# Full-block transposes, stacked low-rank products and bound chunk products in a flow-matching step

## The chip, the cores and the metric

The kernel runs on one core of one Trainium2 chip. A core has five engines that work side by side, each with its own queue in fixed order: TensorE (PE; its weight loads are listed as PEld), VectorE (DVE), ScalarE (ACT), GpSimd (POOL) and SyncE (SP, which here only issues DMAs). Products are written to PSUM, in banks; in this kernel VectorE or ScalarE copies them from there. The metric is the device time of one execution in microseconds, the median of three runs.

## The reference

One layer of a hybrid backbone on 640 tokens (512 latent ones around 128 context ones, d = 2048), all in fp32:

```
h = rmsnorm(x) * (1 + sc1) + sh1
p = h @ w_in                      # 2048 x 5408
r, k, v, wd, ad, gd = split(shift(p[..., :3360]))     # wd, ad: 64 wide, gd: 160 wide
gate  = sigmoid(gd) @ g2                              # 160 x 1024
for d in (forward, backward):
    decay = exp(-exp(-softplus(-(w0[d] + tanh(wd) @ w2[d])) - 0.5))   # 64 x 1024
    a     = sigmoid(a0[d] + ad @ a2[d])                               # 64 x 1024
    S     = S * decay + (S @ a_t) b_t + v_t k_t       # 16 heads, state 64 x 64
    out  += group_norm(S @ r_t) + (r . kd) v
o_a = out * gate
o_b = chunk_gmlp(gelu(p[..., 3360:]))
x = x + g1 * (concat(o_a, o_b) @ w_out)
x = x + g2 * (silu(h2 @ w_ffn_gate) * (h2 @ w_ffn_up)) @ w_ffn_down
```

The two outputs are the normalised streams, a third the final states of the context scan. The recurrence over time is done in chunks of 64 tokens.

## The kernel before

Activations lie with features on the 128 partitions and the 640 tokens along the row; halves of 320 tokens go to one PSUM bank. The wide products are taken as fp32r in three passes: each operand is split into a rounded part (hi, a cast on ScalarE, line 164) and the rest (lo, a subtraction on VectorE, line 165), and hi.hi, hi.lo and lo.hi are added up in PSUM (`win`, lines 186 to 188). Small products stay fp32, and each of those is two MATMUL instructions.

The input projection goes over 42 blocks of 128 output columns. First come the three low-rank blocks (wd and ad, then the two gate blocks), then for each pair of heads p (8 pairs) the blocks r, v and k, with gMLP blocks between some pairs. After each block, `take` copies it out and gives its follow-up work to a Mixer, a list of generators that `between` advances in small steps while the next block's products are written. The yields carry estimated costs; solve and merge (inversion of the small triangular matrices inside the chunks) have Mixers of their own. The framework then puts all instructions of an engine in order at build time: an instruction earlier in the program goes first if its operands are ready by the framework's own timing estimate, and otherwise a later one does. On the chip, each queue runs in that order and waits where the estimate was wrong. DMAs for weights, scratch and results are issued by SP, those of solve and merge by POOL.

`low_rank` (line 467) leaves tanh(wd) in rows 0 to 63 and ad in rows 64 to 127 of `wa`, and the sigmoid of the gate blocks in `gs1` (128 rows) and `gs2` (32 rows). `take_k` (line 514) does, for a pair and for each direction d: the low-rank products of `wl` with `wa` (line 551; h = 0 is w2 with tanh(wd) on rows 0 to 63, h = 1 is a2 with ad on rows 64 to 127), the decays, and the operands R and X of the ten chunks, 64 rows for each of the two heads. Then the products inside the chunks, X by R for each chunk and head (line 613, groups of 4, 4 and 2 chunks, one PSUM tile for each head), which are copied out as GB (ScalarE), GR and GA (VectorE, masked). GR goes to the scratch `d_S`. Then X is transposed for each head (line 630, 64 rows to 128 by 64) and stored to `d_S`, and GA by Z is formed (line 641). All PSUM tiles of this work come from the pool `pk`, tag `g`, two buffers.

The recurrence (`recur`) then walks over the chunks of all pairs in an order written out by hand in hops, the second half of the output projection (`wout_b`) filling in. `finish` normalises a pair's output, forms the gate product (`pmm` with g2, line 1196, its matmul at line 485) and stores the result to `d_o`. The first half of the output projection and the FFN follow, which the change does not touch.

## Time and profile before

| | us |
|---|---|
| median of 3 runs | 3431.64 (3423.08 to 3435.26) |
| profiled execution, span from the first to the last instruction | 3424.7 |
| TensorE busy | 3259.0 (95%) |
| VectorE busy | 2478.4 (72%) |
| ScalarE busy | 1443.5 (42%) |
| GpSimd busy | 1260.5 (37%) |
| mean granted TensorE clock | 0.975 |

The page tells the time between the first and the last instruction of one execution; what lies around it is not in the page, and the runs' times hold both. A matmul's listed length holds its way through the array, so that consecutive ones overlap: what one costs is the distance to the start of the next. "xcount" behind a group is the number of instructions, "64*128" the rows and columns of the array that are used, and "<-" names what ended the wait before it.

### The profile page before, as it was taken

How to read it: one execution, taken by the hardware profiler on the slowest of the kernel's cores; microseconds unless marked ns; L12 is line 12 of the kernel's file. 1: busy time of each engine (PE TensorE's matmuls, PEld its weight loads, DVE VectorE, ACT ScalarE, POOL GpSimd, SP SyncE). 2: the span in 40 equal slices, each digit the busy share in tenths (PEclk: the TensorE clock that was granted, in tenths of full speed). 3: DMA queues.
4: the chain of work that ended last, by engine and by line, in shares of the span. 5: the costliest groups of instructions: out<-in, count | busy, mean ns of one | idle time of the engine just before them, and what ended most of it. 6: DMA issues, size and time to landing. Idle time of an engine off the chain costs nothing.

```text
span 3424.7 us, 72654 instructions
## 1 busy us (share of the span) xinstructions
PE 3259.0 (95%) x28260; PEld 2930.6 (86%) x28260; DVE 2478.4 (72%) x4320; ACT 1443.5 (42%) x3161; POOL 1260.5 (37%) x1090
## 2 busy tenths in 40 slices
PE   6899999999999999989999999999999999999996
PEld 3687778777877887768999999999999999999986
DVE  4547677766866666655788788887888877877787
ACT  3334344444444433324644444444444445443365
POOL 0001112122213112231045656666565554555543
PEclk8899999999999999989999999999999999999998
DMA  8666676677667577635634343434434355543453
GB/s 320 232 189 184 178 194 170 186 189 190 192 179 195 147 236 225 208 111 150 182 109 123 107 127 111 120 115 120 122 105 127 116 166 155 154 145 116 144 169 114
DMA packets 736177, 550.12 MB, mean 161 GB/s; under 512 B 140328, under 2 KB 670008, under 8 KB 727000
## 3 DMA queue, kind: packets, MB, share of 16 engines
q1 hardware_dynamic: 723512, 531.78, 52.2%
q0 software_dynamic: 9984, 13.13, 1.9%
q8 instruction: 222, 3.64, 0.4%
q14 instruction: 123, 1.01, 0.1%
q10 hardware_dynamic: 2336, 0.57, 0.1%
HBM read 436.68 MB, written 111.28 MB: 160 GB/s over the span
## 4 chain that ended last, share of the span: by engine, by line
PE 43%; DVE 5%; issue 4%; DMA 2%; ACT 1%; POOL 0%; DVEq 0%; ACTq 0%; POOLq 0%; SPq 0%
PE P L1502 14%; PE P L1500 13%; PE P L1501 13%; DVE lo L1319 2%; DMA d_os<-act 1%; DVE act L1621 1%; DMA opd<-d_op 1%; PE big L1355 0%; DVE xd L1553 0%; PE big L1353 0%; PE big L1354 0%; DVE out L1856 0%; PE C L1434 0%; PE C L1432 0%; PE C L1433 0%
## 5 line engine op out<-in xcount | busy, mean ns | idle before, releaser
L1502 PE MATMUL P<-xo,lo 128*128 128x320 f32 x2352 | 731.4, 311 | 10.2 <-DVE lo L1319 10.2
L1500 PE MATMUL P<-xo,hi 128*128 128x320 f32 x2352 | 728.3, 310 | 2.1 <-ACT hi L1318 2.1
L1501 PE MATMUL P<-xo,hi 128*128 128x320 f32 x2352 | 727.6, 309 | 0.0
L1319 DVE TENSOR_TENSOR lo<-raw,hi 128x512 fp32r<-128x512 f32 x532 | 567.7, 1083 | 82.8 <-ACT hi L1318 78.0
L1318 ACT CAST hi<-raw 128x512 fp32r<-128x512 f32 x532 | 326.7, 621 | 416.0 <-PE P L1501 322.6
L186 PE MATMUL big<-h_hi,hi 128*128 128x320 f32 x1376 | 452.0, 329 | 8.4 <-ACT hi L164 4.3
L1502 PEld LDWEIGHTS P<-xo,lo 128*128 128x128 f32 x2352 | 442.4, 188 | 17.7 <-DVE lo L1319 17.5
L188 PE MATMUL big<-h_hi,lo 128*128 128x320 f32 x1376 | 441.2, 321 | 4.4 <-DVE lo L165 4.4
L1500 PEld LDWEIGHTS P<-xo,hi 128*128 128x128 f32 x2352 | 442.7, 188 | 3.0 <-ACT hi L1318 2.7
L1501 PEld LDWEIGHTS P<-xo,hi 128*128 128x128 f32 x2352 | 442.4, 188 | 0.0
L187 PE MATMUL big<-h_lo,hi 128*128 128x320 f32 x1376 | 438.9, 319 | 0.5 <-DVE h_lo L343 0.5
L1413 POOL TENSOR_TENSOR raw<-raw 128x512 f32<-128x512 f32 x252 | 409.2, 1633 | 10.9 <-DVE lo L1319 0.9
L1502 PE MATMUL P<-xd,lo 128*128 128x320 f32 x1232 | 384.7, 312 | 17.4 <-DVE lo L1319 17.2
L1500 PE MATMUL P<-xd,hi 128*128 128x320 f32 x1232 | 383.0, 311 | 6.0 <-ACT hi L1318 4.2
L1501 PE MATMUL P<-xd,hi 128*128 128x320 f32 x1232 | 381.6, 310 | 0.0
L165 DVE TENSOR_TENSOR lo<-raw,hi 128x512 fp32r<-128x512 f32 x268 | 184.7, 692 | 235.2 <-ACT hi L164 218.8
L186 PEld LDWEIGHTS big<-h_hi,hi 128*128 128x128 f32 x1376 | 265.0, 193 | 83.2 <-issue 54.1
L164 ACT CAST hi<-raw 128x512 fp32r<-128x512 f32 x268 | 164.9, 618 | 311.2 <-PE big L187 129.5
L188 PEld LDWEIGHTS big<-h_hi,lo 128*128 128x128 f32 x1376 | 265.0, 193 | 20.9 <-issue 8.3
L187 PEld LDWEIGHTS big<-h_lo,hi 128*128 128x128 f32 x1376 | 265.1, 193 | 12.9 <-issue 8.3
L1318 ACT CAST hi<-rawd 128x512 fp32r<-128x512 f32 (+1 forms) x288 | 168.9, 588 | 242.1 <-PE P L1501 206.8
L1413 POOL TENSOR_TENSOR t<-raw 128x512 f32<-128x512 f32 x84 | 135.3, 1611 | 344.8 <-DMA raw<-in_w_ffn_up_dram 334.7
(358 smaller groups left out, 6430.1 us busy)
## 6 DMA issues: line engine op xcount, KB each, us to landing
wt<-in_w_mod_dram SPq DMA_DIRECT2D x96, 1024.0 KB
raw<-in_w_ffn_gate_dram SPq DMA_DIRECT2D x182, 256.0 KB
raw<-in_w_ffn_up_dram SPq DMA_DIRECT2D x182, 256.0 KB
rec<-d_S SPq DMA_DIRECT2D x80, 576.0 KB
raw<-in_w_in_dram SPq DMA_DIRECT2D x172, 256.0 KB
rawd<-in_w_ffn_down_dram SPq DMA_DIRECT2D x128, 256.0 KB
raw<-in_w_out_dram SPq DMA_DIRECT2D x96, 256.0 KB
xd<-d_os SPq DMA_DIRECT2D x66, 320.0 KB
```

Of the source, the lines that this page charges most:

```text
L164: S.copy(hi, raw)
L165: V.tensor_sub(lo, raw, hi.bitcast(F32))
L186: TE.matmul(halves[hf], hi[:, k, :], h_hi[:, kb, s], start=(kb == 0), stop=False)
L187: TE.matmul(halves[hf], hi[:, k, :], h_lo[:, kb, s], start=False, stop=False)
L188: TE.matmul(halves[hf], lo[:, k, :], h_hi[:, kb, s], start=False, stop=(kb == KB - 1))
L1318: S.copy(hi[:, 0:nk], raw[:, 0:nk])
L1319: V.tensor_sub(lo[:, 0:nk], raw[:, 0:nk], hi[:, 0:nk].bitcast(F32))
L1413: G.tensor_tensor(out=o[:, 0:nk], in0=p[:, 0:nk], in1=q[:, 0:nk], op=ALU.subtract)
L1500: TE.matmul(ps, hi[:, k, :], xk[:, 0, :], start=f, stop=False)
L1501: TE.matmul(ps, hi[:, k, :], xk[:, 1, :], start=False, stop=False)
L1502: TE.matmul(ps, lo[:, k, :], xk[:, 0, :], start=False, stop=l)
L1621: V.tensor_sub(lo, src, hi.bitcast(F32))
```

## The change

Four places are changed, all around the head-pair work.

1. The products inside the chunks are issued with the heads alternating (second head first), and each group's instructions are tied to one another in that order (`chain`, an ordering without a semaphore). The PSUM pool gets two tags `g0` and `g1` with one buffer each, in place of one tag with two buffers, so that a head always has the same bank.
2. X is transposed for both heads at once, a full 128 by 128 block per chunk, in groups of 4, 4 and 2 chunks, and stored with one DMA per group.
3. The low-rank products become fp32r products over 128 rows: `waM[:, h]` holds the rounded rows of h in one half and the rest of them in the other half, the weight is loaded twice, once for each half, and is split into `wh` and `wl`; two products then give hi and lo parts of both. The weights are loaded and split for each direction.
4. The gate rows go to the scratch `d_gs`, and come back at the start of the recurrence, split into `gh`, `gl` and `gq` (four copies of the last 32 rows, in two of which the rest stands in place of the rounded value). The gate product is four fp32r products for each half. `J2` (the flipped identity) is made there too, and the solve's input `gi` gets a tile of its own.

```diff
+    d_gs = dp.tile([160, T], F32, name="d_gs")
...
+    def chain(made):
+        for a, b in zip(made, made[1:]):
+            tc.add_manual_dep(b.ins, a.ins.name, mybir.DependencyInfo(
+                mybir.DependencyClass.NoSync, mybir.DependencyReason.DATA), reason="chain")
...
-    wa = bk.tile([P, T], F32, name="wa", bufs=1)
+    waM = bk.tile([P, 2, T], F32R, name="waM", bufs=1)
...
         if b == 24:
-            S.activation(wa[0:64, :], z[0:64, :], AF.Tanh)
-            S.copy(wa[64:128, :], z[64:128, :])
+            S.activation(z[0:64, :], z[0:64, :], AF.Tanh)
+            zl = z.bitcast(F32R)
+            for h in range(2):
+                S.copy(waM[hsl(h), h, :], z[hsl(h), :])
+                V.tensor_sub(zl[hsl(h), :], z[hsl(h), :], waM[hsl(h), h, :].bitcast(F32))
+                nc.sync.dma_start(waM[osl(h), h, :].bitcast(F32), z[hsl(h), :])
         else:
-            dst = gs1 if b == 25 else gs2
-            S.activation(dst, z, AF.Tanh, scale=0.5)
-            V.tensor_scalar(dst, dst, 0.5, 0.5, op0=ALU.mult, op1=ALU.add)
+            S.activation(z, z, AF.Tanh, scale=0.5)
+            V.tensor_scalar(z, z, 0.5, 0.5, op0=ALU.mult, op1=ALU.add)
+            nc.sync.dma_start(d_gs[0:P] if b == 25 else d_gs[P:160], z)
...
-        wl = bk.tile([P, 2, P], F32, tag="wl", name="wl", bufs=1)
-        nc.sync.dma_start(wl[0:64, :, :], w2[0, :, :, p * P:(p + 1) * P].rearrange("d k n -> k d n"))
-        nc.sync.dma_start(wl[64:128, :, :], a2[0, :, :, p * P:(p + 1) * P].rearrange("d k n -> k d n"))
+        def load_wl(d):
+            raw = bk.tile([P, 2, P], F32, tag="GR", name="wlr", bufs=2)
+            for h, w in enumerate((w2, a2)):
+                nc.sync.dma_start(raw[:, h, :], w[0, d, :, p * P:(p + 1) * P].unsqueeze(0).to_broadcast([2, 64, P]))
+            yield 0.5
+            wh, wl = (bk.tile([P, 2, P], F32R, tag=n, name=n, bufs=1) for n in ("wh", "wl"))
+            S.copy(wh, raw)
+            V.tensor_sub(wl, raw, wh.bitcast(F32))
+            o.wl = wh, wl
+            yield 0.5
+        yield from load_wl(0)
...
-                two = [pk.tile([P, HALF], F32, tag="g", name="pwa") for _ in range(2)]
+                two = [pk.tile([P, HALF], F32, tag=f"g{h}", name="pwa") for h in range(2)]
                 for h in range(2):
-                    TE.matmul(two[h], wl[hsl(h), d, :], wa[hsl(h), s], start=True, stop=True)
+                    for i, w in enumerate(o.wl):
+                        TE.matmul(two[h], w[:, h, :], waM[:, h, s], start=i == 0, stop=i == 1)
...
+            if d == 0:
+                yield from load_wl(1)
...
-                two = [pk.tile([P, 4, P], F32, tag="g", name="pG") for _ in range(2)]
-                for cc in range(c0, c1):
-                    for h in range(2):
-                        s = hsl(h)
-                        TE.matmul(two[h][:, cc - c0, :], X[s, cc, :, :].rearrange("p s t -> p (s t)"),
-                                  R[s, cc, :, :].rearrange("p s t -> p (s t)"), start=True, stop=True)
+                two = [pk.tile([P, 4, P], F32, tag=f"g{h}", name="pG") for h in range(2)]
+                chain([TE.matmul(two[h][:, cc - c0, :], X[hsl(h), cc, :, :].rearrange("p s t -> p (s t)"),
+                                 R[hsl(h), cc, :, :].rearrange("p s t -> p (s t)"), start=True, stop=True)
+                       for cc in range(c0, c1) for h in (1, 0)])
...
-            for (c0, c1) in ((0, 8), (8, NCH)):
-                two = [pk.tile([P, 8, CH], F32, tag="g", name="pXT") for _ in range(2)]
+            for (c0, c1) in ((0, 4), (4, 8), (8, NCH)):
+                ps = pk.tile([P, 4, P], F32, tag=f"g{c0 // 4 % 2}", name="pXT")
                 for cc in range(c0, c1):
...
+                    TE.transpose(ps[:, cc - c0, :], X[:, cc, :, :].rearrange("p s t -> p (s t)"), ident)
+                XT = bz.tile([P, 4, P], F32, tag="XT", name="XT", bufs=2)
+                S.copy(XT[:, 0:c1 - c0, :], ps[:, 0:c1 - c0, :])
+                yield 0.2 * (c1 - c0)
+                nc.sync.dma_start(d_S[p, :, d, c0:c1, F_X:F_X + P], XT[:, 0:c1 - c0, :])
...
-    pk = pbx.enter_context(tc.tile_pool(name="pk", bufs=2, space=PSUM))
+    pk = pbx.enter_context(tc.tile_pool(name="pk", bufs=1, space=PSUM))
...
+        gh, gl, gq = (rw.tile([P, T], F32R, name=n) for n in ("gh", "gl", "gq"))
+        nc.sync.dma_start(gl.bitcast(F32), d_gs[0:P])
+        S.copy(gh, gl.bitcast(F32))
+        V.tensor_sub(gl, gl.bitcast(F32), gh.bitcast(F32))
+        gr = rw.tile([P, T], F32, tag="sq", name="gr")
+        for k in range(4):
+            nc.sync.dma_start(gr[32 * k:32 * k + 32, :], d_gs[P:160])
...
-            nc.sync.dma_start(g2a, g2[0, 0:P, p * P:(p + 1) * P])
-            nc.sync.dma_start(g2b, g2[0, P:160, p * P:(p + 1) * P])
+            nc.sync.dma_start(g2r[:, 0, :], g2[0, 0:P, p * P:(p + 1) * P])
+            for k in range(4):
+                nc.sync.dma_start(g2r[32 * k:32 * k + 32, 1, :], g2[0, P:160, p * P:(p + 1) * P])
...
-            pmm([(g2a, gs1), (g2b, gs2)],
...
+            S.copy(g2h, g2r)
+            V.tensor_sub(g2l, g2r[:, 0, :], g2h[:, 0, :].bitcast(F32))
+            V.tensor_sub(g2h[64:128, 1, :], g2r[64:128, 1, :], g2h[64:128, 1, :].bitcast(F32))
...
+                four = ((g2h[:, 0, :], gh), (g2h[:, 0, :], gl), (g2l, gh), (g2h[:, 1, :], gq))
+                for i, (l, r) in enumerate(four):
+                    TE.matmul(ps, l, r[:, s], start=i == 0, stop=i == 3)
```

More of the change, by code (lines that the diff above doesn't have):

```diff
@@ L623, in take_k @@
                     nc.sync.dma_start(d_S[p, :, d, c0:c1, F_G + CH * h:F_G + CH * h + CH], GR[:, 0:c1 - c0, :])
[L625 to L626 removed]
+            for (c0, c1) in ((0, 4), (4, 8), (8, NCH)):
+                ps = pk.tile([P, 4, P], F32, tag=f"g{c0 // 4 % 2}", name="pXT")
                 for cc in range(c0, c1):
[L628 to L636 removed]
+                    TE.transpose(ps[:, cc - c0, :], X[:, cc, :, :].rearrange("p s t -> p (s t)"), ident)
[3 more added lines that the diff above has]
+                nc.sync.dma_start(d_S[p, :, d, c0:c1, F_X:F_X + P], XT[:, 0:c1 - c0, :])
             for c0 in (0, 5):
[L638 removed]
+                ps = pk.tile([P, 5, CH], F32, tag=f"g{1 - c0 // 5}", name="pW0")
                 for cc in range(c0, c0 + 5):
@@ L746, in solve @@
         o = pairs[p]
-        gi = mix[0:80, 0:512].rearrange("p (d a b) -> p d a b", d=2, b=16)
+        gi = gi_
         for d in range(2):
```

39 lines of the change are left out of this document (18 added, 21 removed).

## The prediction

> **What bounds the kernel now.** I read the page first, then busy time by stretch, then TensorE's groups, and last the spacing of single instructions.
>
> ```profile
> span 3424.7 us, 72654 instructions
> PE 3259.0 (95%) x28260; PEld 2930.6 (86%) x28260; DVE 2478.4 (72%) x4320; ACT 1443.5 (42%) x3161; POOL 1260.5 (37%) x1090
> PE 43%; DVE 5%; issue 4%; DMA 2%; ACT 1%; POOL 0%; DVEq 0%; ACTq 0%; POOLq 0%; SPq 0%
> ```
>
> The third line is the head of the chain of waits; what it names is TensorE. The change touches two stretches only, so they are judged by the busy times by stretch. The columns are window, length, busy us of PE, PEld, DVE, ACT and POOL, granted clock, DMA share, GB/s.
>
> ```profile
> 216.00:1180.00 964.00, 923.38 (x10324) 749.65 (x10322) 660.67 (x1321) 409.33 (x892) 197.70 (x304) 0.97 0.68 182
> 1221.00:1510.00 289.00, 288.74 (x4248) 219.56 (x4246) 188.44 (x623) 99.56 (x468) 74.56 (x98) 1.00 0.68 206
> 1510.00:1556.00 46.00, 35.61 (x287) 27.02 (x287) 16.15 (x36) 10.13 (x26) 11.01 (x14) 0.74 0.24 74
> 721.00:794.00 73.00, 70.10 (x998) 57.34 (x997) 60.45 (x122) 35.84 (x78) 17.69 (x28) 1.00 0.68 188
> sum 329.00, PE 317.82 PEld 263.58 DVE 263.10 ACT 150.61 POOL 68.63; mean PE 79.46 PEld 65.89 DVE 65.78 ACT 37.65 POOL 17.16
> ```
>
> 216 to 1180 us is the stretch of the input projection with the head-pair work between its products (the first pair's low-rank product starts it). TensorE is busy 923 of 964 us there, VectorE 661, ScalarE 409. 1221 to 1510 is the recurrence, with TensorE busy 288.74 of 289.00. In both, a microsecond taken from TensorE should come out of the time unless another engine's queue takes its place. The nearest is VectorE: 60.45 of 73 us (83%) in the fourth window. The last line sums the four windows with gMLP blocks (261 to 352, 492 to 573, 721 to 794, 840 to 924), VectorE at 80%.
>
> TensorE's groups in 216 to 1180 (busy us, mean ns, idle before):
>
> ```profile
> L186 PE MATMUL big<-h_hi,hi 128*128 128x320 f32 x1153 | 377.7, 328 | 1.1 <-ACT hi L164 0.6 <-ACT praw L910 0.4
> L613 PE MATMUL pG<-R,X 64*128 64x128 f32 x640 | 88.2, 309 | 14.4 <-DVE X L595 9.1 <-DVE GA L621 4.6 <-ACT GB L618 0.5
> L551 PE MATMUL pwa<-wa,wl 64*128 64x320 f32 x128 | 34.7, 481 | 1.1 <-ACT tha L554 1.1
> L630 PE MATMUL pXT<-ident,X 64*128 64x64 f32 x320 | 29.6, 232 | 1.2 <-DVE GA L621 0.5
> ```
>
> Three of these groups change. An fp32 product leaves two MATMUL records (8 pairs, 2 directions, 10 chunks, 2 heads: 320 products, 640 records at L613), a transpose one. The mean ns is latency; cost is the distance between starts, so I take the timeline of TensorE (start, length, instruction, count):
>
> ```profile
> 610.70 0.30 PE L187 MATMUL big<-h_lo,hi 128*128 128x320 f32 x1
> 610.84 0.31 PE L188 MATMUL big<-h_hi,lo 128*128 128x320 f32 x1
> 610.99 0.31 PE L186 MATMUL big<-h_hi,hi 128*128 128x320 f32 x1
> 611.23 0.71 PE L630 MATMUL pXT<-ident,X 64*128 64x64 f32 x8
> 611.87 0.42 PE L187 MATMUL big<-h_lo,hi 128*128 128x320 f32 x1
> 612.12 0.31 PE L188 MATMUL big<-h_hi,lo 128*128 128x320 f32 x1
> ...
> 622.10 0.81 PE L551 MATMUL pwa<-wa,wl 64*128 64x320 f32 x4
> 622.84 0.42 PE L188 MATMUL big<-h_hi,lo 128*128 128x320 f32 x1
> ```
>
> A full-height fp32r product of 320 columns starts every 0.147 us (610.70 to 610.99 for two). Going into the half-height transposes costs 0.09 more (610.99 to 611.23) and coming out 0.10 more (611.87 to 612.12): each piece of half-height work pays about 0.19 beside its own time.
>
> **Products inside the chunks (L613).** Nothing is removed; the order is bound, the heads alternating. Two groups of the same 16 records:
>
> ```profile
> 380.95 1.16 PE L613 MATMUL pG<-R,X 64*128 64x128 f32 x16
> 382.04 0.42 PE L186 MATMUL big<-h_hi,hi 128*128 128x320 f32 x1
> ...
> 603.58 1.92 PE L613 MATMUL pG<-R,X 64*128 64x128 f32 x16 [0.52 <-DVE GA L621]
> 605.42 0.56 PE L823 MATMUL pM<-TB,GB 32*32 32x32 f32 x22
> ```
>
> One takes 1.09 us from its start to the next, the other 1.84. The fast one can only have its two heads in the array side by side (16 records of 128 columns at 68 ns each, against 115); the slow one has them one after the other. The bound order alternates the heads, so I price every group as the fast one: 32 groups of four chunks at 1.16 busy and 16 of two chunks at 0.7 (an estimate: half the 16 records and the same fill), 48 against the 88.2 in the row: -40. Bounds: 0 if alternating does nothing, -54 if the 14.4 us of idle before the group goes too. I take -40, since 88.2/640 = 138 ns a record says that most groups run the slow way.
>
> **Low-rank products (L551).** Removed: 64 half-height fp32 products, as 128 records. A whole set of four costs 0.74 (622.10 to 622.84) and 0.19 of switching, 0.93. Its length is 0.81, so 34.7 busy us are 43 pieces, some sets being split: 43 x 0.93 = 40. Added: 128 full-height fp32r products of 320 columns, of the very form of the projection, so at 0.147 and without switching: 19. That is -21; bounds -11 (if they came only as 32 whole sets, 30) and -21.
>
> The Trainium skill speaks against this one (TensorEngine Tiling (Array Packing), When to Use Tiling): two contractions of at most 64 rows can share the array as two row tiles, which stacking to 128 rows gives up. The trace has that sharing (four records in 0.74), and by it alone a stacked pass would cost twice a shared one. The halved passes and the switching still win by the rows above, so the sum does not change sign; by that rule's full factor of two the term would be near zero, and the total 21 us smaller.
>
> **Transposes of X (L630).** Removed: 320 half-height ones. Eight take 0.64 (611.23 to 611.87) and 0.19 of switching: 40 such pieces, 33. Added: 160 of 128 by 128, a form that stands in the trace elsewhere:
>
> ```profile
> 330.38 0.31 PE L188 MATMUL big<-h_hi,lo 128*128 128x320 f32 x1
> 330.53 0.60 PE L508 MATMUL pvt<-ident,zv 128*128 128x128 f32 x4
> 330.88 0.39 PE L186 MATMUL big<-h_hi,hi 128*128 128x320 f32 x1
> 331.11 0.31 PE L187 MATMUL big<-h_lo,hi 128*128 128x320 f32 x1
> ```
>
> Four take 0.35, entered without delay, and the product behind them is late by 0.08: 0.108 each, 17 in all. -16; bounds -12 (20 us if each came alone at 0.125) and -20.
>
> **Gate product (L485, from L1196).** Removed per half: two fp32 products.
>
> ```profile
> 1336.27 0.81 PE L485 MATMUL pmm<-gs,g2a 128*128 128x320 f32 x2
> 1337.01 0.80 PE L485 MATMUL pmm<-mix,g2b 32*128 32x320 f32 x2
> 1337.74 0.42 PE L988 MATMUL big<-oh,hi 128*128 128x320 f32 x1
> ...
> 1534.62 0.47 PE L1355 MATMUL big<-oh,lo 128*128 128x320 f32 x1
> 1534.89 1.27 PE L485 MATMUL pmm<-gs,g2a 128*128 128x320 f32 x2
> ...
> 1541.59 0.63 PE L1353 MATMUL big<-oh,hi 128*128 128x320 f32 x1 [0.64 <-DVE bv L1197]
> ```
>
> 1.47 us (1336.27 to 1337.74) and 0.10 on the way out; added are four fp32r products, 0.59. 14 halves of pairs 0 to 6: 14 x 0.98 = 14. The last pair stands at the end of the stretch, where nothing covers it and the spacing is 0.27 (1534.62 to 1534.89): 6.70 now (1534.89 to 1541.59), eight times 0.27 and two waits of about 0.75 for VectorE after it, 3.7: -3. Bounds of the two: -10 and -19.
>
> **What is added beside TensorE.** Rows for the prices:
>
> ```profile
> L164 ACT CAST hi<-raw 128x512 fp32r<-128x512 f32 x149 | 91.4, 618 | 138.9 <-PE big L187 102.5 <-DMA raw<-in_w_in_dram 24.5 <-issue 7.5
> L620 DVE TENSOR_TENSOR GR<-pG,mask 128x256 f32<-128x256 f32 (+1 forms) x96 | 35.8, 373 | 40.9 <-ACT GB L618 19.8 <-DMA d_S<-GR 17.1 <-ACT R L574 2.0
> L521 SPq DMA_DIRECT2D wl<-in_a_dram x8: 596/607/617, 139.4 to 990.5; - x8
> ACT hi L164 <- DMA raw<-in_w_in_dram: 24.5, 12, 7.7
> PE pG L613 <- DVE X L595: 9.1, 9, 4.1
> PE pG L613 <- DVE GA L621: 4.6, 7, 1.1
> ```
>
> Splitting the low-rank weights: 16 casts of 128x256 on ScalarE (half of 618, 0.31) and 16 subtractions on VectorE (about 0.37), 5 and 6 us; ScalarE gives 16 XT copies of the small kind back. Splitting the low-rank rows and the gate (some 30 operations of under 0.8 us each) is spread over both stretches. I cost these at nothing: the work that hides them is the projection's own products, as VectorE is free for 303 of 964 us and ScalarE for 555; without that cover they are 11 us. DMAs issued by SP, at 0.61 each: 16 more for weights, 16 fewer for XT, 4 for the low-rank rows, 29 more in the recurrence (18 us of SP there, in front of record loads that are called several hops ahead): nothing, or up to 5 if one record is late.
>
> What I do charge is three waits. ScalarE now has a cast that waits for a weight DMA, and behind it in the same queue stand the projection's own casts, for which TensorE waits: such a wait on the projection's loads took 2.0 us (24.5/12), 16 of them 33, mostly covered by the two pieces loaded ahead: +4 of 0 to 33. A bound group starts with the head whose banks come free last, and stands at the head of TensorE's queue when the order, fixed at build time, puts it too early: today that wait costs 1.0 (9.1/9) or 0.7 (4.6/7) when it happens, and 48 groups can meet it: +8 of -14 to +48. And in the four dense windows VectorE has to go from 80% to near 87%: +5 of 0 to 25.
>
> **Sum.** -40 -21 -16 -14 -3 = -94; +4 +8 +5 = +17. The profiled span becomes 3424.7 - 77 = 3348. The median of the runs, 3431.6, lies 6.9 above that span, so 3354.6, put down as 3354.
>
> **Rivals.**
>
> VectorE becomes the bound in the dense windows. Speaking for it: 83% in 721 to 794, where a share of 77 in 964 would leave 60.8 busy of 67 us, 91%. Against: over the whole stretch it would be 667 of 887, 75%. If the four windows gained nothing, 329/964 of 77 is lost, 26, with half as much again for the queues around them: -94 +17 +39, 3394.
>
> The binding does nothing: two tiles from two buffers were already two banks, so a bank per head changes no collision, and alternating could be undone by one head waiting. Against: 380.95 is the same form at full rate. Without that term -37: 3395.
>
> The time hardly moves: TensorE's fixed order fills the saved time with waits for the head pair's chain on VectorE and ScalarE, which did not get shorter. For: the row of idle before L613 (14.4) is such a wait. Against: it is 1.6% of the stretch. That gives 3425 to 3440.
>
> Slower: the bound group blocks TensorE's queue. Before, one head could start while the other's copies ran; now both wait behind the slower, with the projection's products behind them. The price is a wait of 4.1 (the longest row) at the 32 later groups, 131, so 94 gained less 131: 3424.7 + 37 + 6.9 = 3469. It decides from 94/32 = 2.9 us a group. Against: the mean is 1.0 today, and products of the projection stand between most groups.
>
> **How the numbers follow.** What a measurement of this kernel can tell is about 0.3%, 10 us. Forecast (3325 to 3375) 0.55; VectorE 0.13; binding without effect 0.10; hardly moves 0.07; slower 0.08; more than the sum, because idle at L613 goes and fewer pieces pay the switching, 0.07 (-94 -14 -9: 3315). The range that leaves out about 2 in 10 runs from 3318 to 3410; the likeliest case's own is 3325 to 3375. Faster 0.85, same 0.07, slower 0.08.
>
> **What would show it.** L613 as 48 pieces of 16 or 8 records at 1.09 and 0.6 us; L551's successor at 0.147 between projection products with no late neighbour; 160 transposes of 128x128 at 0.108; the gate at 0.59 a half. Wrong, if TensorE's idle time in the first stretch grows from 41 us to over 80, if waits of TensorE for GA or X, or of ScalarE for the weight DMA, grow by tens of us, or if the stretch from the end of the recurrence to the end of the span changes by more than a few.

## The result and the profile after

| | before | after |
|---|---|---|
| median of 6 runs each, us | 3433.45 (3423.08 to 3449.84) | 3413.49 (3406.70 to 3419.84) |
| ratio | | 0.9948 (95%: 0.9926 to 0.9971) |
| span of the profiled execution, us | 3424.7 | 3413.2 |

The change gains 20 us, where 77 were forecast. The head of the page of the kernel after, and the share of each engine in its chain of waits:

```profile
span 3413.2 us, 72346 instructions
PE 3189.6 (93%) x28100; PEld 2905.1 (85%) x28100; DVE 2512.9 (74%) x4357; ACT 1451.5 (43%) x3172; POOL 1251.9 (37%) x1090
PE 50%; DVE 6%; issue 5%; DMA 3%; POOL 1%; ACT 1%; DVEq 0%; SPq 0%; ACTq 0%; POOLq 0%
```

TensorE lost 69 us of busy time (3259.0 to 3189.6), and the span lost 11.5. Busy time by stretch of the kernel after (window, length, busy us of PE, PEld, DVE, ACT and POOL, granted clock, DMA share, GB/s):

```profile
216.00:1163.00 947.00, 858.85 (x10103) 717.57 (x10102) 655.77 (x1327) 412.75 (x890) 190.93 (x303) 0.97 0.69 187
1218.00:1495.00 277.00, 276.68 (x4226) 217.96 (x4225) 189.57 (x632) 98.82 (x470) 74.60 (x98) 1.00 0.71 214
1495.00:1536.00 41.00, 30.03 (x283) 26.26 (x281) 15.91 (x37) 10.11 (x27) 10.86 (x14) 0.75 0.23 74
```

The projection stretch was 960.5 us long (first low-rank product to last product of the projection) and is 947.2; TensorE's waits in it rose from 40.1 to 88.2. The recurrence is full in both, and went from 285.7 to 275.1. The hand-over between the two grew from 44.3 to 54.1; of these 9.8 us, 5.5 are waits of TensorE (2.8 to 8.3). From the end of the recurrence to the FFN 3.6 came off. The FFN's code did not change; it took 1679.3 us in the profile of before, 1686.2 here and 1681 to 1695 in the profiles below, so that its 6.9 more here are within the spread of single executions.

TensorE's groups in the projection stretch after:

```profile
L629 PE MATMUL pG<-R,X 64*128 64x128 f32 x640 | 49.6, 290 | 22.6 <-DVE X L618 11.5 <-DVE GA L638 10.8
L645 PE MATMUL pXT<-ident,X 128*128 128x128 f32 x160 | 25.3, 284 | 8.0 <-DVE GA L638 5.9 <-ACT XT L647 1.0 <-ACT A__1127 L797 0.8
L568 PE MATMUL pwa<-waM,wh 128*128 128x320 f32 x64 | 25.1, 395 | 4.7 <-DVE mx L774 4.1 <-ACT Z L656 0.4 <-ACT wh L532 0.3
L568 PE MATMUL pwa<-waM,wl 128*128 128x320 f32 x64 | 20.9, 329 | 7.1 <-DVE wl L533 7.1
```

The first row is what was forecast, 49.6 busy for 88.2. The idle parts are what was not: 22.6, 8.0 and 11.8 us, where the answering rows of before have 14.4, 1.2 and 1.1. What TensorE waited for in this stretch (sum, times, longest):

```profile
PE pG L629 <- DVE X L618: 11.5, 10, 4.0
PE pG L629 <- DVE GA L638: 10.8, 18, 1.9
PE psp L740 <- DVE vt L727: 7.6, 3, 3.2
PE pwa L568 <- DVE wl L533: 7.1, 2, 3.7
PE pm L872 <- DMA wt<-in_w_mod_dram: 6.7, 8, 1.7
PE pXT L645 <- DVE GA L638: 5.9, 6, 3.2
PE big L184 <- DVE lo L161: 4.8, 3, 4.3
```

No single wait is the answer: the longest row is 11.5 us. One of them can be followed to its root, and it shows what a wait really costs. TensorE in the kernel after (start, length, instruction):

```profile
428.76 0.41 PE L568 MATMUL pwa<-waM,wh 128*128 128x320 f32 x1
429.01 0.31 PE L182 MATMUL big<-h_hi,hi 128*128 128x320 f32 x1
432.98 0.41 PE L568 MATMUL pwa<-waM,wl 128*128 128x320 f32 x1 [3.66 <-DVE wl L533]
...
435.55 0.47 PE L183 MATMUL big<-h_lo,hi 128*128 128x320 f32 x1
435.82 0.47 PE L184 MATMUL big<-h_hi,lo 128*128 128x320 f32 x1
436.09 0.47 PE L182 MATMUL big<-h_hi,hi 128*128 128x320 f32 x1
...
437.11 0.31 PE L182 MATMUL big<-h_hi,hi 128*128 128x320 f32 x1
437.26 0.30 PE L183 MATMUL big<-h_lo,hi 128*128 128x320 f32 x1
```

VectorE at the same time:

```profile
423.91 0.49 DVE L546 TENSOR_SCALAR ssq<-pmm 128x320 f32<-128x320 f32 x1 [0.90 <-PE pmm L491]
429.93 0.16 DVE L772 TENSOR_TENSOR mx<-mx,gi 80x2 f32<-80x2 f32 x1 [5.53 <-DMA gi<-dd]
...
432.51 0.41 DVE L533 TENSOR_TENSOR wl<-wlr,wh 128x256 fp32r<-128x256 f32 x1
```

VectorE stood 5.53 us at the first row of another pair's substitution (the rows that invert the small triangles, one after the other), whose input `gi` was still in transfer; behind it in the same queue stood the subtraction `wl` that this change added, and TensorE's queue stood at the product that reads `wl`. Then the clock, in three windows of the same view as above:

```profile
429.00:433.00 4.00, 0.34 (x3) 0.08 (x2) 2.79 (x13) 0.00 (x0) 0.00 (x0) 1.00 0.92 251
434.00:435.00 1.00, 1.00 (x4) 0.62 (x3) 0.64 (x3) 0.00 (x0) 0.00 (x0) 0.50 0.63 223
437.00:441.00 4.00, 4.00 (x29) 2.95 (x29) 3.97 (x6) 3.96 (x7) 1.58 (x1) 1.00 0.33 76
```

After the wait the granted clock is 0.50 for 3.4 us, and products of the projection start every 0.27 us (435.55 to 435.82) and not every 0.15 (437.11 to 437.26). So this wait of 3.7 us cost 1.7 more, half of those 3.4. I therefore split each projection stretch in three: TensorE's waits; time lost to the clock (slices of about 10 us, length times one less the granted clock, summed); and the rest, which is its work at full clock (slow time inside a wait is in both of the first two: 1 us in these two kernels, up to 7 in those below). Before: 40.1 + 29.0 + 891.4. After: 88.2 + 24.0 + 835.1. The work fell by 56 us, the waits took back 48.

Not all of the clock's loss stands behind a long wait. Taking a slow piece as begun by a wait when it begins between the wait's start and 0.6 us after its end, waits of over 2 us began 6.8 of the 29.0 before and 11.9 of the 24.0 after; 18.8 and 8.5 began with no wait of 0.3 us or more beside them, and why is open.

### The profile page after: what moved, and what is told of

It is laid out like the page before. It is cut to its first block, busy times and chain, and to the rows that moved or that the text cites. A ratio compares the mean times of both kernels' runs of the same rounds, so it can differ in the third digit from the quotient of the medians.

```text
span 3413.2 us, 72346 instructions
## 1 busy us (share of the span) xinstructions
PE 3189.6 (93%) x28100; PEld 2905.1 (85%) x28100; DVE 2512.9 (74%) x4357; ACT 1451.5 (43%) x3172; POOL 1251.9 (37%) x1090
## 4 chain that ended last, share of the span: by engine, by line
PE 50%; DVE 6%; issue 5%; DMA 3%; POOL 1%; ACT 1%; DVEq 0%; SPq 0%; ACTq 0%; POOLq 0%
PE P L1541 13%; PE P L1539 13%; PE P L1540 13%; DVE lo L1358 2%; PE big L1002 2%; DMA d_os<-act 1%; PE big L1003 1%; PE big L1004 1%; PE u_ps L1149 1%; PE y_ps L1105 1%; PE s_ps L1170 1%; PE pO L1217 1%; DVE act L1660 1%; PE big L1394 1%; PE big L1392 1%
## 5 line engine op out<-in xcount | busy, mean ns | idle before, releaser
L1358 DVE TENSOR_TENSOR lo<-raw,hi 128x512 fp32r<-128x512 f32 x532 | 585.9, 1120 | 64.1 <-ACT hi L1357 60.0
L1541 PEld LDWEIGHTS P<-xo,lo 128*128 128x128 f32 x2352 | 442.4, 188 | 18.9 <-DVE lo L1358 18.8
L1541 PE MATMUL P<-xd,lo 128*128 128x320 f32 x1232 | 385.1, 313 | 17.8 <-DVE lo L1358 17.5
L161 DVE TENSOR_TENSOR lo<-raw,hi 128x512 fp32r<-128x512 f32 x268 | 185.7, 696 | 182.0 <-ACT hi L160 179.9
```

Of the source, the lines that this page charges most:

```text
L161: V.tensor_sub(lo, raw, hi.bitcast(F32))
L1358: V.tensor_sub(lo[:, 0:nk], raw[:, 0:nk], hi[:, 0:nk].bitcast(F32))
L1541: TE.matmul(ps, lo[:, k, :], xk[:, 0, :], start=False, stop=l)
```

## The experiments

One profile each for the columns from "stretch" on (us; "work", "waits" and "clock" as just defined). Ratios are to the kernel before, on the same chip, with their 95% interval.

| kernel | median | ratio | stretch | work | waits | clock | hand-over |
|---|---|---|---|---|---|---|---|
| before | 3433.45 | | 960.5 | 891.4 | 40.1 | 29.0 | 44.3 |
| after | 3413.49 | 0.9948 (0.9926 to 0.9971) | 947.2 | 835.1 | 88.2 | 24.0 | 54.1 |
| bind_only | 3446.04 | 1.0043 (1.0027 to 1.0060) | 967.6 | 859.9 | 70.0 | 37.7 | 47.1 |
| xt_only | 3426.82 | 0.9984 (0.9967 to 1.0002) | 962.0 | 871.6 | 51.1 | 39.3 | 43.5 |
| lowrank_gate | 3425.46 | 0.9974 (0.9959 to 0.9989) | 954.8 | 875.1 | 54.1 | 25.6 | 50.1 |
| gate_only | 3426.62 | 0.9982 (0.9964 to 1.0001) | 967.7 | 889.2 | 42.6 | 35.9 | 48.2 |
| unbound | 3414.12 | 0.9951 (0.9932 to 0.9969) | 945.4 | 857.9 | 55.1 | 32.4 | 53.9 |
| pe_plus | 3434.45 | 1.0016 (1.0000 to 1.0032) | 963.6 | 866.9 | 69.4 | 27.3 | 53.5 |
| pe_minus | 3405.51 | 0.9933 (0.9917 to 0.9949) | 945.8 | 792.7 | 101.8 | 51.3 | 45.6 |
| dve_chain_minus | 3404.47 | 0.9928 (0.9910 to 0.9946) | 940.5 | 832.3 | 79.1 | 29.1 | 52.0 |
| after_decoupled | 3429.40 | 0.9992 (0.9975 to 1.0009) | 965.0 | 831.7 | 90.6 | 42.7 | 51.3 |
| before_decoupled | 3444.37 | 1.0046 (1.0024 to 1.0068) | 974.6 | 885.4 | 48.3 | 41.0 | 44.2 |
| half_mod_loads | 3392.74 | 0.9881 (0.9856 to 0.9906) | 925.6 | 831.7 | 68.2 | 25.7 | 49.5 |
| short_solve | 3382.53 | 0.9845 (0.9816 to 0.9873) | 926.4 | 836.1 | 71.5 | 18.8 | 44.0 |
| after_lo_pool | 3441.23 | 1.0032 (1.0013 to 1.0051) | 967.7 | 834.1 | 96.1 | 37.5 | 54.8 |
| before_lo_pool | 3490.88 | 1.0197 (1.0169 to 1.0224) | 1008.1 | 894.2 | 59.2 | 54.7 | 42.7 |
| after_solve_offchain | 3386.46 | 0.9889 (0.9863 to 0.9915) | 929.1 | 839.3 | 67.6 | 22.2 | 44.0 |
| after_spread | 3424.11 | 0.9981 (0.9962 to 1.0000) | 949.2 | 829.6 | 88.9 | 30.7 | 53.7 |
| after_hold55 | 3439.36 | 1.0014 (1.0000 to 1.0027) | 989.0 | 842.1 | 100.8 | 46.2 | 43.7 |
| before_hold55 | 3459.08 | 1.0069 (1.0044 to 1.0095) | 991.5 | 890.6 | 44.6 | 56.3 | 44.2 |

**The parts alone.** bind_only is the kernel before with the bound groups (and the tags `g0`, `g1`):

```diff
-                for cc in range(c0, c1):
-                    for h in range(2):
-                        TE.matmul(two[h][:, cc - c0, :], ...)
+                chain([TE.matmul(two[h][:, cc - c0, :], ...)
+                       for cc in range(c0, c1) for h in (1, 0)])
```

> Kernel before with part 1 alone (the products inside the chunks bound in groups with alternating heads, a bank per head). Theory A, TensorE's own time sets the projection stretch: the pG products take about 40 us less and the time falls by 30 to 40 us. Theory B, the loop of hand-overs between TensorE, ScalarE and VectorE sets the stretch: the pG products also take 40 us less, TensorE's idle time there grows by 30 us or more, and the time moves by less than 10 us. Theory C, the binding itself blocks TensorE's queue: the time rises by 10 us or more, with the idle time in front of pG and pXT.

xt_only is the kernel before with full-block transposes of X:

```diff
-                    for h in range(2):
-                        TE.transpose(two[h][:, cc - c0, :], X[s, cc, :, :]..., ident[s, s])
+                    TE.transpose(ps[:, cc - c0, :], X[:, cc, :, :]..., ident)
```

> Kernel before with part 2 alone (full-block transposes of X, three groups, PSUM pool as before). Theory A: TensorE's transposes take 8 us less and about as much again goes in switching, so the time falls by 10 to 16 us. Theory B: within 6 us of before. Theory C (binding blocks the queue) says nothing different from A here.

lowrank_gate is the kernel after with the loops of these two parts put back to those of before:

> The changed kernel with parts 1 and 2 undone: stacked low-rank products, the gate product and the bank per head remain. Theory A: 20 us from the low-rank products and 14 from the gate, the time falls by 25 to 35 us. Theory B: only the gate's 10 to 14 us in the recurrence show, and the projection stretch stays or grows by the wait for the split weights (up to 11 us), so the time falls by 3 to 14 us. Theory C: as A.

gate_only is the kernel before with the gate rows stored, loaded back and split, and the four fp32r gate products:

```diff
-            pmm([(g2a, gs1), (g2b, gs2)], ...)
+                four = ((g2h[:, 0, :], gh), (g2h[:, 0, :], gl), (g2l, gh), (g2h[:, 1, :], gq))
+                for i, (l, r) in enumerate(four):
+                    TE.matmul(ps, l, r[:, s], start=i == 0, stop=i == 3)
```

> Kernel before with part 4 alone (gate rows through the scratch, four fp32r products for a half). The recurrence keeps TensorE busy all the time, so all theories say the same: the recurrence and what follows it up to the FFN fall by 12 to 17 us, the projection stretch stays, the time falls by 8 to 17 us.

Each part takes its work off TensorE (31.5, 19.8 and 16.3 us in the column "work" for the first three; the gate's is in the recurrence, which fell by 9.1 us to 276.6). In the stretch, waits and clock take it back: xt_only and lowrank_gate came out as theory B said, and gate_only gained 6 us and not the 8 to 17 that all theories gave it, since its stretch came out 7 us longer at 7 us more of lost clock. The binding alone makes the kernel slower, as theory C said of the time; its waits rise by 30 us, as theory B said, and its clock loses 9 more. That makes 7.1 us of stretch, and 2.8 of hand-over; the rest of its loss lies outside what the change touches (the FFN took 1695 us in this profile). TensorE's waits in that kernel:

```profile
PE pm L862 <- DMA wt<-in_w_mod_dram: 16.5, 12, 3.5
PE pG L616 <- DVE GA L625: 10.3, 12, 2.7
```

The first is the wait for the modulation's weights, which the change does not touch; in before it is 4.4. The parts' ratios do not add up: 1.0043, 0.9984 and 0.9974 would multiply to 1.0001, and all of it together is 0.9948.

**The binding undone, TensorE's work added and taken away.** unbound is the kernel after with the heads one after the other in each chunk and no binding, each head still in its own bank:

> The changed kernel without the binding (pG products in the kernel before's order, free to be interleaved; everything else of the change stays). Theory A, TensorE's time sets the stretch: pG back up by about 40 us of TensorE, the projection stretch 30 us or more longer than in the changed kernel. Theory B, hand-overs set it: TensorE's idle time falls from 88 us by about as much as pG rises, the stretch within 10 us of the changed kernel's 947. Theory C, binding blocks the queue: the stretch shorter than the changed kernel's by 10 us or more.

pe_plus adds four first products to each block and half of the projection (the sum starts again behind them):

```diff
             for k in range(4):
                 kb = 4 * q + k
+                for _ in range(4 if kb == 0 else 0):
+                    TE.matmul(halves[hf], hi[:, k, :], h_hi[:, kb, s], start=True, stop=True)
```

> The changed kernel with 4 more copies of the first product of each block and half in the projection (overwritten by the real one, so the result stays): 42 us more of TensorE in the projection stretch, 8 us more ahead of it, on no other engine. Theory A: the stretch grows by about 42 us. Theory B: by less than 15 us, the rest goes into what is idle time now (88 us).

pe_minus leaves out one product of twelve, that of the weights' low half for one of four row blocks:

```diff
-                TE.matmul(halves[hf], lo[:, k, :], h_hi[:, kb, s], start=False, stop=(kb == KB - 1))
+                if k != 2:
+                    TE.matmul(halves[hf], lo[:, k, :], h_hi[:, kb, s], start=False, stop=(kb == KB - 1))
```

> The changed kernel with one of the twelve products of each quarter left out in the projection (the lo.hi product of every third row block, so the projection is less exact): 42 us less of TensorE in the projection stretch. Theory A: the stretch falls by 30 to 42 us. Theory B: by less than 15 us, and TensorE's idle time grows by the rest.

dve_chain_minus puts a multiplication by a constant in the place of the reciprocal on the way to the keys (L552; leaves out their norm):

```diff
-            V.reciprocal(ssq[:, s], ssq[:, s])
+            V.tensor_scalar_mul(ssq[:, s], ssq[:, s], 0.018)
```

> The changed kernel with the reciprocal in the head-pair work replaced by a plain scaling, so that the normalisation of kk is only roughly its own: 16 times about 1.8 us less on VectorE, 29 us, and as much off the chain of each pair. Theory A: the stretch within 8 us of 947. Theory B: it falls by 15 to 29 us.

These settle the first question. With 42 us of TensorE's work taken away (835.1 to 792.7) the stretch is 945.8, as long as with it: 13.6 went into waits and 27.3 into the clock. Of these 27.3, 20.5 are slow pieces begun by waits of over 2 us, and the low clock is no accident of one execution: over the whole kernel it was 0.965 to 0.972 in the four runs of pe_minus, and 0.975 to 0.979 in the six of the kernel after. With 31.8 us added the stretch grows by 16.4, nearer to theory B's 15 than to A's 42. Undoing the binding adds 22.8 us of work and changes nothing, 945.4. What pe_minus gains in the median lies outside the stretch: hand-over -8.5, and -6.3 ahead of it, where the projection's first three blocks stand. In dve_chain_minus 22 us fewer on VectorE (656 to 634, where 29 were expected) took 6.7 off, within the 8 of theory A and not the 15 to 29 of theory B. So in this stretch, a microsecond of TensorE is worth between nothing and a half.

**What sets the waits: buffers, transfers, substitution.** after_decoupled issues the transfer of a weight piece three pieces ahead (`prefetch`), and its copy to `hi` and the subtraction for `lo` one piece ahead (`convert`):

```diff
-        prefetch(n + LEAD)
+        prefetch(n + 3)
+        convert(n + 1)
```

> The changed kernel, but the weight pieces of the projection are handled in two steps: the transfer of a piece is issued three pieces ahead, and its copy to fp32r (ScalarE) and the rest (VectorE) one piece ahead instead of two, so that the copy never waits for TensorE to let go of a buffer. Theory H (the hold: ScalarE's queue stands at the copy for the piece after next until TensorE has finished the piece before, 90.8 us of idle in the projection stretch of the changed kernel are put down to it, and the head pair's work stands behind it, so each piece has a length that TensorE's own work does not set): the 90.8 us fall under 25, TensorE's gaps in the stretch fall from 88 to 40 to 65, the stretch from 947 to 905 to 930 us, and the time from 3413 to 3375 to 3400. Theory D (transfers, the modulation's quads of 1 MB above all, set the length) and theory E (the substitution and merge on VectorE and POOL's queue): stretch within 6 us of 947, time within 8 of 3413.

before_decoupled is the same edit on the kernel before:

> The same edit on the kernel before. H: the stretch falls from 960 to 940 to 955, since TensorE has 40 us of gaps there and not 88; the difference between this run and the changed kernel with the same edit grows from 16 us to 30 to 60, and the sum of the prediction (-77) comes out for most of its part. D and E: within 8 us of 3430, and the difference stays at 10 to 22.

half_mod_loads and short_solve:

```diff
                 if kb + 1 < KB:
-                    quad = load_mod(g, kb + 1)
+                    if kb % 2:
+                        quad = load_mod(g, kb + 1)
```

> The changed kernel with every second quad of the modulation's weights not loaded (each loaded quad is used for two products in its place; leaves out half of the modulation's weights): 32 MB of about 178 MB of transfers less in the projection stretch, the same work on TensorE. D: the stretch falls by 40 us or more (32 MB at the stretch's mean of 186 GB/s would be 170 us). H and E: it falls by 0 to 12 us.

```diff
-        for i in range(1, 16):
+        for i in range(1, 8):
```

> The changed kernel with the substitution stopped after 7 of its 15 rows (leaves out the rows after the seventh): about 60 of its 91 us of VectorE's time in the stretch go, all of them on the way from a pair's products to its merge. E: the stretch falls by 35 to 60 us. H: VectorE is one of the engines in the ring, so by its share so far (6.7 us for 29 us) 8 to 18 us. D: 0 to 6 us.

The hold falls. Both kernels got slower by about 15 us, and ScalarE's copies waited for TensorE more, 117.7 us where 90.8 were to fall under 25; in after_decoupled:

```profile
L923 ACT CAST hi<-raw 128x512 fp32r<-128x512 f32 x141 | 86.4, 619 | 135.3 <-PE big L183 117.7 <-DMA raw<-in_w_in_dram 10.3 <-DVE gq L680 2.8
```

It seems that ScalarE is so far ahead of TensorE in the written order that it stands there in any case. The other two each took 21 us off the stretch at the same work for TensorE, one by transfers and one on the way through VectorE, between what two theories wanted (0 to 12 and 40 or more; 8 to 18 and 35 to 60). Both touch the wait seen at 429.93; VectorE's wait for `gi` in the kernel after:

```profile
DVE mx L772 <- DMA gi<-dd: 28.9, 8, 5.5
```

In half_mod_loads:

```profile
DVE mx L772 <- DMA gi<-dd: 12.0, 7, 3.1
```

In short_solve it is 13.2, and 14.6 in before, where that input lies in the tile `mix`. It is not the whole answer: it is 16.7 in after_spread and 17.8 in unbound, whose stretches are as long as that of after.

**VectorE's load, the length of the chain, the order.** after_lo_pool moves every second subtraction of the weights' low half to GpSimd (`pool` is true there):

```diff
-        V.tensor_sub(lo, raw, hi.bitcast(F32))
+        (G if pool else V).tensor_sub(lo, raw, hi.bitcast(F32))
```

> The changed kernel with the subtraction that makes the low half of every second weight piece of the projection moved from VectorE (0.691 us each, 143 in the stretch) to GpSimd: about 49 us of VectorE's time in the stretch are gone and nothing else is taken out. Theory V (VectorE's throughput where it is full: TensorE's waits are for VectorE's results in 58 of its 88 us): stretch 10 to 25 us shorter than 947, TensorE's waits for GA, X, wl and vt fall by a third or more. Theory L (the length of a pair's chain, products to substitution to merge, and not VectorE's load): within 6 us of 947, since a subtraction that is not on that chain was taken out. If GpSimd is slow at it (2 us or more) and its queue holds up the small transfers of the substitution, the stretch grows instead.

> The same edit on the kernel before. V: TensorE has only 40 us of waits there, so the stretch falls by 0 to 10 us from 960, and the difference between the changed kernel and this one grows from 16 us to 25 to 40: the part of the predicted gain that VectorE held back comes out. L: both move alike and the difference stays at 12 to 20.

after_solve_offchain lets the merge start after seven rows and does the other eight behind it:

```diff
-        for i in range(1, 16):
+        for i in range(1, 8):
             row(i, True)
...
         mixM.add(merge(p, d2), 18.0)
+        for i in range(8, 16):
+            row(i, False)
```

> The changed kernel with the merge of a pair started after 7 of the 15 rows of the substitution, and the other eight rows worked out all the same, behind it, into a place that nobody reads (leaves out the rows after the seventh, as the run with the short substitution did, at the same VectorE time as the changed kernel). V: VectorE's work is back, so the 21 us that the short substitution gained are lost again: stretch 940 to 952. L: the chain is as short as there: stretch 922 to 932.

after_spread has 16 for 12 in the planner's divisor:

```diff
-ADIV = 12.0
+ADIV = 16.0
```

> The changed kernel with the head pairs' steps spread more evenly between the projection's products (the divisor of what is left goes from 12 to 16, with the old end of each block's work kept), so that less of it comes in a row. If the written order is what makes TensorE meet unready operands (theory O): its gaps change by 15 us or more in either direction, and the stretch by 8 or more. V and L: within 8 us of 947.

Moving work to GpSimd made both kernels slower. The subtraction takes 1456 ns there and 691 on VectorE, but the larger harm seems to be in its queue, in after_lo_pool:

```profile
L161 POOL TENSOR_TENSOR lo<-raw,hi 128x512 fp32r<-128x512 f32 x72 | 104.8, 1456 | 268.5 <-ACT hi L160 262.4 <-PE big L184 4.6 <-PE big L183 1.0
```

GpSimd stood 262 us for ScalarE's copies, with the substitution's transfers behind them. So this run says nothing on VectorE's throughput. The edit cost the kernel before more than the kernel after (3491 against 3441), and why is open. after_solve_offchain is the clean one: VectorE's time is back (660.76 us in a window of 928, where short_solve had 615.50 in one of 940), and of the 21 us gained 18 stay, as theory L said. So it is not VectorE's load that counts here, but the shorter way from a pair's products to its merge, or the merge's earlier place that comes with it. The even spread left the waits at 88.9 and the stretch at 949.2: no effect there, in an execution that was 7 us faster than this kernel's median.

**The place of the merge in the order.** Starting the merge early also put its products earlier in TensorE's queue. The last two runs change only that, in the kernel after and in the one before:

```diff
-HOLD = 68
+HOLD = 55
```

> The changed kernel with one number of the written order changed: a pair's merge is taken up 55 counts of the projection's products (three each) after its transfers were issued, and not 68, which puts its products on TensorE's queue within a few counts of where they stood in the run whose substitution ended after 7 rows (386 against 384, 546 against 544, 662 against 670, 802 against 802, 914 against 922). All the work is done. Theory O (the place of the merge in the written order makes the difference, and neither VectorE's time nor the length of the chain): stretch 924 to 936, hand-over 44 to 48, time 3382 to 3395. Theory L (the chain must really be shorter: here the merge meets operands that come 20 us later than there): stretch 940 to 955, time 3405 to 3420, with TensorE's waits for the merge's operands (pblk, pM, pT) up by 5 us or more.

> The same number in the kernel before. If the order had been fitted to the old products and the gain of the change went into waits at the misfit (O): within 8 us of 3430 (3422 to 3438), so that the difference to the changed kernel with 55 is 30 to 55 and not 16. If 55 is simply the better number for both: 3400 to 3415, and the difference stays at 12 to 25, the gain of the change still held back by something else. L: no change, 3425 to 3438, and the difference as it was.

The same place without the shorter chain costs 42 us of stretch, more than either theory gave it. TensorE's wait for the merge's operands in after_hold55, and no other row of that view is over 10:

```profile
PE pblk L811 <- DMA TB<-d: 24.6, 13, 5.2
```

In the kernel after, that row is:

```profile
PE pblk L811 <- DMA TB<-d: 0.9, 1, 0.9
```

So at 68 the merge's operands come just in time, the earlier place gains only together with the shorter chain, and the length of the chain (products, transfer of `dd`, transfer of `gi`, substitution, transfers of `d` and `TB`) is a limit beside TensorE. The hand-over did come back, to 43.7, which suggests that the 9.8 us there go with the place of the last merges. The kernel before lost 31 us in the stretch, which no theory had, but little of it in waits (44.6); its clock lost 56.3, of which 18.8 were begun by waits of over 2 us. That the order had been fitted to the old products, so that the gain went into the misfit, is not borne out by this number: the difference between the two kernels with 55 is 19.7, not 30 to 55.

No kernel that does all the work was faster than the changed one; unbound equals it.

## Why the prediction was wrong, step by step

The sizes of the first three parts are distances from one start to the next, without waits and without what half clock cost. What it costs to go into and out of half-height work falls on the projection's products beside a piece and is counted apart; "in all" holds both.

- **Products inside the chunks: mis-sized.** Forecast -40. As they stand, the distances sum to 87.5 us before and 46.9 after, -40.6, but that this meets the forecast is luck: 4.0 of the 87.5 are waits, and 9.7 are half clock that fell on these products in that execution. One such group (granted clock 0.50) lists 3.27 where the two groups of the prediction list 1.16 and 1.92:

```profile
1077.27 3.27 PE L613 MATMUL pG<-R,X 64*128 64x128 f32 x16 [0.24 <-DVE GA L621]
```

Without both, 73.7 became 45.2, -28.5 (bind_only has 45.4, unbound 74.0), and -31 in all. The bound form is as forecast; the 88.2 busy of the old row were put down to the order of the heads alone. A bound group of four chunks takes 1.09 from its start to the next, one of two 0.64:

```profile
408.59 1.16 PE L629 MATMUL pG<-R,X 64*128 64x128 f32 x16 [0.52 <-DVE GA L638]
409.68 0.41 PE L182 MATMUL big<-h_hi,hi 128*128 128x320 f32 x1
...
414.04 0.71 PE L629 MATMUL pG<-R,X 64*128 64x128 f32 x8 [0.28 <-DVE GA L638]
414.68 0.42 PE L184 MATMUL big<-h_hi,lo 128*128 128x320 f32 x1
```

- **Low-rank products: mis-sized.** Forecast -21; 31.7 became 24.1, -7.6. The old ones came in 42 pieces of 0.75, and the 0.19 of switching stood on their neighbours, as forecast: the projection's product ahead takes 0.23 to the next start and the one behind 0.26, where 0.147 is usual. In before:

```profile
351.79 0.31 PE L188 MATMUL big<-h_hi,lo 128*128 128x320 f32 x1
352.02 0.81 PE L551 MATMUL pwa<-wa,wl 64*128 64x320 f32 x4
352.76 0.42 PE L186 MATMUL big<-h_hi,hi 128*128 128x320 f32 x1
353.02 0.31 PE L187 MATMUL big<-h_lo,hi 128*128 128x320 f32 x1
```

In the kernel after:

```profile
386.49 0.31 PE L182 MATMUL big<-h_hi,hi 128*128 128x320 f32 x1
386.64 0.31 PE L568 MATMUL pwa<-waM,wh 128*128 128x320 f32 x1
386.79 0.31 PE L568 MATMUL pwa<-waM,wl 128*128 128x320 f32 x1
386.93 0.31 PE L183 MATMUL big<-h_lo,hi 128*128 128x320 f32 x1
```

That takes another 7 off the projection's products, so -15 in all. The old side, 40, was right; the new one was priced too low. Of the new products 68 of 128 take about 0.15, as in these lines, but 56 take about 0.25: 10 at half clock, 29 beside a product of another form (428.76 above is one), and 17 between the projection's own products, where the trace shows no reason. By the Trainium skill's rule quoted there (TensorEngine Tiling (Array Packing), When to Use Tiling: the sharing that stacking gives up) the term would have been near zero; the trace lies between that and the forecast, nearer to the forecast.
- **Transposes: mis-sized.** Forecast -16; 26.2 became 18.3, -7.9, and -11 in all. The old ones cost 33 with their switching, as priced. Of the new ones 91 of 160 take 0.11, as priced, but others up to 0.28, so that they cost 22 with their switching and not 17.
- **Gate: right in kind.** Forecast -14 for 14 halves; their distances sum to 19.8 before and 8.9 after, -10.9. Twelve of the halves lie in the recurrence, which came out 10.6 shorter. Behind a product at full clock the four stand as priced:

```profile
1300.73 0.31 PE L1235 MATMUL pG<-gh,g2h 128*128 128x320 f32 x1
1300.88 0.31 PE L1235 MATMUL pG<-gl,g2h 128*128 128x320 f32 x1
1301.03 0.31 PE L1235 MATMUL pG<-gh,g2l 128*128 128x320 f32 x1
1301.17 0.31 PE L1235 MATMUL pG<-gq,g2h 128*128 128x320 f32 x1
1301.32 0.32 PE L1003 MATMUL big<-ol,hi 128*128 128x320 f32 x1
```

- **Last pair: right.** 6.70 to 3.99 (1519.62 to 1523.61), forecast 3.7; the stretch behind the recurrence is 3.6 shorter. Gate and last pair together are -14, inside their bounds of -10 and -19.
- **So of the -94, about 70 are there** (56.3 of work in the projection stretch, 10.6 in the recurrence, 3.6 behind it). Of the 57 us by which the forecast missed the median's 20, about 24 are sizes: half clock and waits read as work (10), the new low-rank products and transposes (11), the gate (3). The other 33 are what waits took back beyond the 17 charged; the profiles have 48 more of waits in the stretch, 5 less of lost clock and 10 more of hand-over.
- **The step that failed** is the sentence on the bound: "In both, a microsecond taken from TensorE should come out of the time unless another engine's queue takes its place". It holds in the recurrence (0.3 us of waits) and not in the projection stretch, where a share of 96% was read as the bound. bind_only and xt_only show it on the kernel before: 31.5 and 19.8 us fewer on TensorE, and a stretch 7.1 and 1.5 longer. pe_minus shows it on the kernel after, with products that the change does not touch: 42 us fewer, 1.4 gained there. The waits rose by 48, spread over X, GA, vt, wl, wt and lo. Of the three waits charged, ScalarE's casts held TensorE for 0.3 us (`wh`) and 0.4 (`hi`); the row of the bound group rose by 8.2 (14.4 to 22.6), as charged; and VectorE's load was not what counted (after_solve_offchain). The new wait on VectorE was for `wl`, in a queue that stood for a transfer. It is the rival "The time hardly moves", which had 0.07, and its mark (waits over 80) is the one that was met; its time, 3425 to 3440, was too high, since the recurrence and the tail kept their 14.
- **Left out altogether:** half clock, and with it the price of a long wait beyond its length. The prediction used the spacing of 0.27 at the last pair without asking why it is not 0.147; the granted clock is 0.50 there. Beyond the 10 us named above this is not what the total missed by, since the column "clock" fell by 5.
- **What stays open:** what begins the slow pieces that have no wait beside them; how the 48 us divide among the chain to the merge, the transfers and the waits for X and GA; that shortening the chain or halving the modulation's loads gives 18 to 21 each was shown on the kernel after alone.

## What to carry to other kernels

A share of 95% on one engine says that it is the bound only if the others have slack at the places where the work comes off: before pricing a saving, ask what the next instructions on that engine read, and how long before it they are ready now. An order written out in counts of one engine's products is a clock: when that engine gets faster, every transfer and chain that was given a number of counts gets less time. A cheap test is to leave out some of the engine's work, unrelated to the change, and see whether the time moves.

## What the runs showed of the hardware

A long wait of TensorE often costs more than its length. In the projection stretches of all twenty profiles, the granted clock fell to 0.50 (between the wait's start and 0.6 us after its end) at 49 of 65 waits over 3 us and at 48 of 105 of 2 to 3 us, but at 10 of 87 of 1.5 to 2 us and 24 of 869 of 0.3 to 1.5 us; it stayed there for 3.4 us or a multiple of it (in the kernel after ten times 3.4 and twice 6.8). These waits are not the whole of the column "clock", which is 19 to 56 us of a stretch and as large as many of the differences between the kernels: of its 707 us in the twenty stretches, 304 were begun by waits of over 2 us, and 287 began with no wait of 0.3 us or more beside them; single pieces of 14 to 31 us make it vary. The Trainium skill (TensorE: Matmul & The Clock Gate, HAM oscillation) sets the limit for idle gaps at about 3.4 us. The trace agrees with the 3.4 us as the unit of the slow time, but half clock already followed nearly half of the waits of 2 to 3 us.

Going into half-height work and out of it costs the full-height products beside it 0.09 and 0.11 us: in before, with the clock full and no wait, the product ahead of a low-rank piece took 0.237 to the next start on the mean and the one behind it 0.254, against 0.147.

The other surprise is how little of an order can be moved: 13 counts in the place of each pair's merge cost 42 us, in a stretch in which 42 us of products could be left out for nothing.
